# A decoder layer on one core: GpSimd's long arithmetic moved to VectorE, and the delta rule's inverse begun from blocks of 16 rows

## The chip, the core and the metric

The kernel runs on 1 core of one Trainium2 chip. Its engines are TensorE (PE; PEld is its weight load), VectorE (DVE), ScalarE (ACT), GpSimd (POOL), and SyncE (SP), which here issues nearly all DMAs. What counts is the device time of one execution in microseconds (us), the median of several runs. Beside it stands one execution taken by the hardware profiler, from which all rows below come.

## What is computed

One layer of a decoder trunk, 512 tokens of width 1024, in float32: a SwiGLU feed-forward network (FFN), a mixer of two head groups (forgetting attention, "fox", 8 heads of 64, and a gated delta rule, 4 heads of 128), cross-attention to 256 memory tokens, and a second FFN; RMS norms stand before and after each part. The part that the change touches most is the delta rule. Cut to that:

```python
qkv = causal_conv_silu(concat([gq, gk, gv]), conv_w)      # y[t] = sum_i x[t-3+i] * w[i], then silu
decay = exp(where(incl, g[..., :, None] - g[..., None, :], -inf))
L = where(strict, einsum('bhncd,bhnsd->bhncs', k_beta, k) * decay, 0.0)
A = L + eye(CHUNK)                                        # lower triangular, ones on the diagonal
u = triangular_solve(A, v_beta); w = triangular_solve(A, k_beta * exp(g)[..., None])
# scan over the chunks of tokens, with the state S of each head:
v_new = u - w @ S;  o = (q * exp(g)) @ S + attn_intra @ v_new;  S = S * exp(g_last) + k_tail.T @ v_new
```

The kernel takes chunks of 128 tokens and forms T = (I + L)^-1 and its transpose X.

## The kernel before

**Tiling.** Activations stand transposed, [channel, token], in blocks of 128 rows by 512 tokens. A float32 product is made of three passes: every weight block of 128 x 1024 is loaded into a `raw` buffer (three of them), split into a high part `wh` (ScalarE) and a low part `wl` (VectorE, one subtraction with both inputs in SBUF), and TensorE multiplies high by high, high by low and low by high. `wblock` and `wsplit` do that; with `nblock[1] = 2`, which is set from the delta rule to the end of the fox heads and again in the memory attention, every second `wl` is made by GpSimd.

**The mixer.** First come the gates (`zr`, `gw`, `yd`: a softplus worked out by some twenty small VectorE instructions on 128 x 64) and the keys of the four delta heads. `conv` makes the causal convolution of a block: ScalarE writes the first tap (`cy`) and the last (`cth`), VectorE adds two taps, GpSimd adds `cth`, ScalarE takes the tanh, VectorE the product (`co`). Then L of each head is worked out (`L`).

**The inverse.** T is built from 32-row diagonal blocks. L goes to a DRAM buffer (`dl`), its diagonal blocks come back one block to a partition (`Lb`: 4 heads x 4 chunks x 4 blocks = 64 partitions), and 31 steps of substitution on VectorE (a product into `Wb`, a subtraction from `Tb`) invert all of them at once. The blocks go to a DRAM buffer (`dt`), come back in place as `T`, and `inverse` doubles them twice on TensorE: from 32 to 64 rows (products of 32 x 32) and from 64 to 128 (products of 64 x 64), with `Qs` between the two products of a step. `qv` makes queries and values of a head, `scan` runs over its chunks. `PLAN` lists these stages; `F0` are the fox values.

**The order.** Nothing is issued in the order of the text. `Issue` keeps every instruction with what it reads and writes, gives each an assumed duration (in `add`) and an assumed delay to those that wait for it (`AFTER`), places them forwards and backwards ten times, and hands each engine one fixed order. An assumed duration takes no account of what other engines do at that time. SyncE's DMAs are ordered in the same way.

**Norms.** `rstd_of` makes the factor of a row block by one instruction on VectorE, one on ScalarE and a power on GpSimd.

Of the kernel before, what the change touches and what calls it, by code (L numbers as in the profile page):

```python
# [16 lines left out]
P = 128  # L17
# [9 lines left out]
NSLOT = 51  # L27
# [11 lines left out]
class Issue:  # L39
    """The order in which the engines issue.  # L40

    Every instruction is kept with what it reads and writes. At the end they are placed on the
    engines by a rough cost, backwards and forwards by turns, of those ready the most urgent
    first, and each engine gets its instructions in that order (as dependencies that need no
    semaphore).
    """

    # from the end of an instruction to the start of one that waits for it: on the same engine,
    # on the tensor engine, on another
# [45 lines left out]
    def cells(self, x):  # L95
        """name, pieces touched, rows, free size"""
# [22 lines left out]
    def add(self, ins, unit, op, fp32):  # L119
# [4 lines left out]
        for group, cells_of, size_of in ((ins.ins, reads, sizes[0]), (ins.outs, writes, sizes[1])):  # L124
            for x in group:
# [5 lines left out]
                if name.startswith("psum"):  # L131
                    # one after another on a bank
# [51 lines left out]
    def keep(self, unit):  # L184
        """the last instruction stays behind the last kept one of its engine"""
# [4 lines left out]
    def place(self, edges, waits, urgency, clock=False):  # L190
        """start of each instruction, on each unit the most urgent ready one first"""
# [68 lines left out]
class _Issuer:  # L260
    """an engine whose instructions are kept"""
# [19 lines left out]
def tile_decoder_layer(  # L281
# [23 lines left out]
    cid32: bass.AP,  # L305
# [14 lines left out]
    # slots of [128, 512], handed out by hand  # L320
# [20 lines left out]
    def move(src, dst, n=None):  # L341
        """free slots from one ring to another"""
# [14 lines left out]
    def bank(*ids):  # L357
        """the next PSUM bank of a ring of banks"""
# [20 lines left out]
    # that of some instructions stays as written  # L379
# [49 lines left out]
    nblock = [0, 0]  # L429
# [13 lines left out]
    # the first loads, in the order in which they are needed  # L443
# [28 lines left out]
    def prenorm(src, g, dst):  # L472
        """rms_norm of a block of 128 rows, transposed and split into dst(half, part)."""
# [78 lines left out]
    def residual_epilogue(gidx, weight, nxt, final=False):  # L552
        """evac callback: h += weight * rms_norm(product) * gain; then nxt(t)."""
# [165 lines left out]
    # ================= mixer =================  # L719
# [9 lines left out]
    cr = issue.tile(pool, [P, 11], F32, tag="cr", name="cr")  # L729
# [41 lines left out]
    # gates: each of four groups of 32 rows holds a decay logit, two forget logits and a beta  # L771
    # logit, four rows each, and the same again for the low part of the weights; the logarithms are worked out by token, [128 tok, chunk, group, kind]
# [57 lines left out]
    def aug(src):  # L830
        """rows (-hi, -lo, 1, 1) and (1, 1, hi, lo) of a logarithm, whose product is its difference"""
# [15 lines left out]
    # per-token columns [128 tok, chunk, head]  # L847
# [25 lines left out]
    def conv(blk, ps):  # L873
# [18 lines left out]
    nblock[1] = 2  # L892
# [4 lines left out]
    # the 32-row diagonal blocks of each head go through DRAM, a block to a partition and back  # L897
# [674 lines left out]
```

## Time and profile before

| | |
|---|---|
| median of 3 runs | 1224.75 us (1223.94 to 1227.4) |
| profiled execution, first to last instruction | 1222.4 us |
| median less that span | 2.35 us |
| TensorE busy | 1192.9 us (98%), 6078 products |
| VectorE busy | 642.7 us (53%) |
| ScalarE busy | 493.0 us (40%) |
| GpSimd busy | 128.6 us (11%) |
| mean granted clock of TensorE | 0.995 |

The stages by the time in the span: FFN 1 to about 375 us, the mixer's gates, keys and delta rule to about 555, the fox heads to about 640, output projection and memory attention to about 880, FFN 2 to the end. A line of the profile that is named L270 is the recording helper of the program, so instructions are told apart by the names of what they write and read. Busy time on TensorE counts a product from its start to its modelled end, and products overlap; the distance from one start to the next is what a product costs.

### The profile page before, as it was taken

Reading aid. Unit: us, or ns where it says so; the run is one execution under the profiler, and the core shown is the slowest. Engines: PE = TensorE matmul, PEld = TensorE weight load, DVE = VectorE, ACT = ScalarE, POOL = GpSimd, SP = SyncE. Lnnn points to the kernel's source line nnn. Section 1 sums busy time; section 2 is a strip of 40 time slices with the busy share of each in tenths; the row PEclk is TensorE's granted clock in tenths of the full one; section 3 lists DMA queues with packets and bytes.
Section 4 is the critical chain, followed back from the end, with each engine's and each line's share of the span. In section 5 each row is a group of like instructions: output and inputs, shape, how many; then the busy total and the mean of one; then the engine's idle time right before and its main releaser. Section 6 shows DMA issues by size and latency. Waiting matters only on the chain.

```text
span 1222.4 us, 15630 instructions
## 1 busy us (share of the span) xinstructions
PE 1192.9 (98%) x6078; PEld 1002.6 (82%) x6078; DVE 642.7 (53%) x1152; ACT 493.0 (40%) x1024; POOL 128.6 (11%) x121
## 2 busy tenths in 40 slices
PE   7999999999999899899999999999999999999997
PEld 7888888888888687788787888888988888888886
DVE  5655455442327979469975744546634334342323
ACT  5323223222226564368974644435422323222221
POOL 1000000000001432222020442012000000000000
PEclk9999999999999999999999999999999999999999
DMA  5332322333333231211214253222432332333321
GB/s 192 122 100 90 103 88 102 103 103 104 109 101 104 87 113 57 91 54 54 73 60 164 91 181 118 79 67 65 125 103 88 102 97 93 104 107 100 102 71 69
DMA packets 41753, 120.32 MB, mean 98 GB/s; under 512 B 9424, under 2 KB 9680, under 8 KB 41680
## 3 DMA queue, kind: packets, MB, share of 16 engines
q1 hardware_dynamic: 41168, 119.20, 30.9%
q8 instruction: 47, 0.77, 0.3%
q0 software_dynamic: 512, 0.13, 0.1%
q14 instruction: 26, 0.21, 0.1%
HBM read 114.73 MB, written 4.46 MB: 98 GB/s over the span
## 4 chain that ended last, share of the span: by engine, by line
PE 87%; DVE 7%; DMA 2%; issue 2%; ACT 2%; SPq 0%; POOL 0%; DVEq 0%; POOLq 0%; ACTq 0%
PE psum L270 87%; DVE Wb L270 1%; DVE Tb L270 1%; DMA mr<-in_mem_dram 1%; DVE wl L270 1%; DVE gw L270 1%; DMA raw<-in_wkvk_dram 1%; DVE co L270 1%; DVE xn L270 1%; DVE cy L270 0%; SPq L270 0%; DMA h<-in_x_dram 0%; DVE smalls L270 0%; DVE pt L270 0%; DVE h L270 0%
## 5 line engine op out<-in xcount | busy, mean ns | idle before, releaser
L270 PE MATMUL psum<-xt,wh 128*128 128x512 f32 (+1 forms) x2064 | 599.4, 374 | 0.3 <-ACT wh L270 0.2
L270 PEld LDWEIGHTS psum<-xt,wh 128*128 128x128 f32 x2064 | 373.6, 190 | 63.5 <-ACT wh L270 0.5
L270 ACT ACTIVATE wh<-raw 128x1024 fp32r<-128x1024 f32 (+1 forms) x202 | 213.0, 1056 | 526.0 <-PE psum L270 293.3
L270 PE MATMUL psum<-xt,wl 128*128 128x512 f32 (+1 forms) x1016 | 376.6, 375 | 0.8 <-DVE wl L270 0.7
L270 DVE TENSOR_TENSOR wl<-raw,wh 128x1024 fp32r<-128x1024 f32 (+1 forms) x176 | 216.3, 1230 | 275.8 <-ACT wh L270 275.2
L270 PEld LDWEIGHTS psum<-xt,wl 128*128 128x128 f32 x1016 | 190.9, 190 | 32.7 <-DVE wl L270 1.2
L270 PE MATMUL psum<-wh,hh 128*128 128x512 f32 x352 | 137.1, 390 | 0.0
L270 PE MATMUL psum<-wl,hh 128*128 128x512 f32 x352 | 137.1, 390 | 0.0
L270 PE MATMUL psum<-wh,hl 128*128 128x512 f32 x352 | 137.0, 389 | 0.0
L270 POOL TENSOR_TENSOR smalls<-smalls,mhalf 128x1 f32<-128x1 f32 (+1 forms) x38 | 26.5, 700 | 789.8 <-ACT smalls L270 784.0
L270 PEld LDWEIGHTS psum<-wh,hh 128*128 128x128 f32 x352 | 66.1, 188 | 13.8
L270 PEld LDWEIGHTS psum<-wh,hl 128*128 128x128 f32 x352 | 66.1, 188 | 13.6
L270 PEld LDWEIGHTS psum<-wl,hh 128*128 128x128 f32 x352 | 66.1, 188 | 13.6
L270 POOL TENSOR_TENSOR wl<-raw,wh 128x1024 fp32r<-128x1024 f32 x26 | 63.7, 2450 | 120.8 <-ACT wh L270 110.2
L270 PE MATMUL psum<-wh,xt 128*128 128x512 f32 x128 | 43.5, 409 | 0.4 <-DVE q L270 0.4
L270 DVE SCALAR_TENSOR_TENSOR hv<-s,psum 128x512 f32<-128x512 f32 x22 | 15.1, 688 | 53.7 <-PE psum L270 53.5
L270 DVE TENSOR_TENSOR tu<-psum,rb 128x512 f32<-128x512 f32 x22 | 15.2, 692 | 53.4 <-PE psum L270 53.3
L270 DVE TENSOR_TENSOR fg<-psum,gbc 128x512 f32<-128x512 f32 x32 | 22.0, 688 | 37.1 <-ACT u L270 37.1
L270 DVE TENSOR_TENSOR tg<-psum,rb 128x512 f32<-128x512 f32 x22 | 15.2, 692 | 44.5 <-PE psum L270 44.5
L270 ACT ACTIVATE u<-psum 128x512 f32<-128x512 f32 x32 | 19.0, 593 | 41.4 <-PE psum L270 41.4
L270 ACT ACTIVATE hh<-hv 128x512 fp32r<-128x512 f32 x44 | 27.4, 623 | 16.2 <-DVE hv L270 16.2
L270 DVE TENSOR_TENSOR hl<-hv,hh 128x512 fp32r<-128x512 f32 x44 | 30.1, 685 | 1.5 <-ACT hh L270 1.5
(232 smaller groups left out, 1431.3 us busy)
## 6 DMA issues: line engine op xcount, KB each, us to landing
raw<-in_f2gu_dram SPq DMA_DIRECT2D x44, 512.0 KB
raw<-in_f1gu_dram SPq DMA_DIRECT2D x43, 512.0 KB
raw<-in_f1d_dram SPq DMA_DIRECT2D x22, 512.0 KB
raw<-in_f2d_dram SPq DMA_DIRECT2D x22, 512.0 KB
raw<-in_wmt_dram SPq DMA_DIRECT2D x21, 512.0 KB
gbc<-in_gains_dram SPq DMA_DIRECT2D x16, 256.0 KB
raw<-in_wmn_dram SPq DMA_DIRECT2D x8, 512.0 KB
raw<-in_wout_dram SPq DMA_DIRECT2D x8, 512.0 KB
```

The lines of the kernel that those rows point to most:

```text
L270: r = call(*args, **kw)
```

## The change

- `wblock` gives every low part to VectorE; GpSimd makes none.
- `conv` drops ScalarE's `cth` of the last tap and GpSimd's addition, and VectorE adds three taps instead of two.
- The products with the output gate (`gx`, sixteen of 128 x 128) go from GpSimd to VectorE.
- `rstd_of` drops ScalarE's instruction: VectorE adds both sums and the constant in one.
- The substitution works on blocks of 16 rows, 32 to a head, 128 partitions in all: 15 steps instead of 31, on at most 64 elements a partition instead of 256. `Lb` and `Tb` are moved by one DMA a head instead of four, with rows of 64 bytes instead of 128; `dl`, `dt` and `T` are moved in rows of 512 bytes instead of 2048.
- `inverse` doubles once more, from 16 to 32 rows, ahead of the old steps: per head 16 products into `qp`, a masked copy on VectorE, 28 products into `xp` and 7 subtractions on VectorE.
- In `add`, one-pass products are assumed 10.7 ns longer, four-pass products on at most 32 rows half as long, and the scan instruction on VectorE twice as long an element. Three more slots of SBUF are handed out.

```diff
-            cost = max(size * passes * 0.41667, cols * 0.8333) + 2.6
+            cost = max(size * passes * 0.41667, cols * 0.8333) + (13.3 if passes == 1 else 2.6)
+            if passes == 4 and rows <= 32:
+                cost /= 2
-            cost = 68 + size * (6.3 if op == "reciprocal" else 0.521 if single else 1.042) + 61 * scalars
+            each = {"reciprocal": 6.3, "tensor_tensor_scan": 2.04}.get(op, 0.521 if single else 1.042)
+            cost = 68 + size * each + 61 * scalars
...
-        V.tensor_scalar(z0, s0, EPS, None, ALU.add)
-        A.activation(z, z0, AF.Identity, bias=s1)
+        V.tensor_scalar(z, s0, s1, EPS, ALU.add, ALU.add)
...
-        nblock[0] += 1
-        return wsplit(wload(ap), G if nblock[1] and nblock[0] % nblock[1] == 0 else V)
+        return wsplit(wload(ap))
...
-        A.activation(th[:, 0 : S - 3], ps[:, 0 : S - 3], AF.Copy, scale=w4[:, 0:1])
-        for i in (2, 1):
+        for i in (2, 1, 0):
             d = 3 - i
             V.scalar_tensor_tensor(y[:, d:], ps[:, : S - d], w4[:, i : i + 1], y[:, d:], ALU.mult, ALU.add)
-        G.tensor_tensor(y[:, 3:], y[:, 3:], th[:, 0 : S - 3], ALU.add)
...
-        Q.dma_start(rows_of(dl[hh]), L)
-        for c in range(NT):
-            p0 = 16 * hh + 4 * c
-            Q.dma_start(Lb[p0 : p0 + 4], blocks_of(dl[hh], c))
+        Q.dma_start(rows_of(dl[hh]), by_chunk(L))
+        Q.dma_start(Lb[32 * hh : 32 * hh + 32], blocks_of(dl[hh]))
...
-    for j in range(31):
-        n = [64, 31 - j, j + 1]
+    for j in range(15):
+        n = [P, 15 - j, j + 1]
...
+        quarters = [slice(32 * i, 32 * i + 32) for i in range(4)]
+        qp = pg()
+        for c in range(NT):
+            for b in quarters:
+                mm(qp[b, 32 * c : 32 * c + 32], ck(L, c)[b, b], ck(X, c)[b, b], start=True, stop=True)
+        V.tensor_tensor(c3(Qs[:, 0:P]), c3(qp[:, 0:P]), low16[:, None, :].to_broadcast([P, NT, 32]), ALU.mult)
+        xp = pg()
+        for c in range(NT):
+            for b in quarters:
+                mm(xp[b, 32 * c : 32 * c + 32], ck(T, c)[b, b], Qs[b, 32 * c : 32 * c + 32], start=True, stop=True)
+            for b in quarters[0:3]:
+                mm(xp[b, P + 32 * c : P + 32 * c + 32], Qs[b, 32 * c : 32 * c + 32], ck(T, c)[b, b], start=True, stop=True)
+        for i, b in enumerate(quarters):
+            V.tensor_tensor(c3(X)[b, :, b], c3(X)[b, :, b], c3(xp[:, 0:P])[b], ALU.subtract)
+            if i < 3:
+                V.tensor_tensor(c3(T)[b, :, b], c3(T)[b, :, b], c3(xp[:, P : 2 * P])[b], ALU.subtract)
...
-            G.tensor_tensor(ck(gx, c), ck(oraw[hh], c), ck(sgz[c], hh), ALU.mult)
+            V.tensor_tensor(ck(gx, c), ck(oraw[hh], c), ck(sgz[c], hh), ALU.mult)
```

The three places at which the order is looked at follow. On VectorE, the end of the gates (`gw` up to `yd`, which TensorE transposes next); before:

```order
L270 SCALAR_TENSOR_TENSOR cy_458_3102<-psum_64,cw_2744,cy_458_3102 128x511
L270 SCALAR_TENSOR_TENSOR gw_430_2964<-gw_430_2964 128x64
L270 SCALAR_TENSOR_TENSOR cy_458_3102<-psum_64,cw_2744,cy_458_3102 128x510
L270 SCALAR_TENSOR_TENSOR gw_430_2964<-gw_430_2964 128x64 x7
L270 TENSOR_TENSOR gw_430_2964<-gw_430_2964 128x64
L270 TENSOR_TENSOR gw_430_2964<-gw_430_2964,coef_2750 128x64
L270 SCALAR_TENSOR_TENSOR co_460_3110<-cth_459_3104,cy_458_3102 128x512
L270 COPY yd_431_2988<-gw_430_2964 128x16x16
```

and after:

```order
L273 SCALAR_TENSOR_TENSOR gw_430_2952<-gw_430_2952 128x64
L273 TENSOR_TENSOR wl_518_3513<-raw_516_3510,wh_517_3512 128x1024
L273 SCALAR_TENSOR_TENSOR gw_430_2952<-gw_430_2952 128x64
L273 SCALAR_TENSOR_TENSOR cy_487_3320<-psum_64,cw_2732,cy_487_3320 128x511
L273 TENSOR_TENSOR gw_430_2952<-gw_430_2952 128x64
L273 SCALAR_TENSOR_TENSOR cy_487_3320<-psum_64,cw_2732,cy_487_3320 128x510
L273 TENSOR_TENSOR gw_430_2952<-gw_430_2952,coef_2738 128x64
L273 SCALAR_TENSOR_TENSOR co_478_3219<-cth_477_3214,cy_476_3212 128x512
L273 COPY yd_431_2976<-gw_430_2952 128x16x16
```

The seven dependent `gw` instructions that stood in a row have convolutions and weight splits between them, and the convolutions run further ahead (three heads of keys and the first query). On GpSimd, the first stage of the mixer, from the cleared buffer `zb` on; before:

```order
L270 MEMSET zb_448_3040 128x512
L270 TENSOR_TENSOR cy_450_3050<-cy_450_3050,cth_451_3052 128x509
L270 TENSOR_TENSOR wl_487_3353<-raw_485_3350,wh_486_3352 128x1024
L270 TENSOR_TENSOR cy_458_3102<-cy_458_3102,cth_459_3104 128x509
L270 TENSOR_TENSOR wl_503_3465<-raw_501_3462,wh_502_3464 128x1024
L270 TENSOR_TENSOR smalls_63<-smalls_63,mhalf_66 128x4
```

and after:

```order
L273 MEMSET zb_448_3028 128x512
L273 TENSOR_TENSOR smalls_63<-smalls_63,mhalf_66 128x4 x4
L273 DMA k2_618_4530<-ao_603_4448 4x512
L273 TENSOR_TENSOR ro_538_3755<-smalls_63,mhalf_66 128x4
L273 TENSOR_TENSOR ro_546_3897<-smalls_63,mhalf_66 128x4
```

What is left on GpSimd there are powers on four columns, memory fills and DMA issues. On TensorE, the first products of the inverse (X, L, Qs and T of a head; `wh`, `wl` with `xt` are the fox values); before:

```order
L270 MATMUL psum_64<-wh_572_4046,xt_390_2564 128x512
L270 MATMUL psum_64<-X_534_3692,L_457_3092 32x32 x4
L270 MATMUL psum_64<-wh_575_4076,xt_389_2563 128x512
L270 MATMUL psum_64<-wl_576_4077,xt_389_2563 128x512
L270 MATMUL psum_64<-wh_575_4076,xt_390_2564 128x512
L270 MATMUL psum_64<-wh_575_4076,xt_389_2563 128x512
```

and after:

```order
L273 MATMUL psum_64<-wh_565_4016,xt_387_2556 128x512
L273 MATMUL psum_64<-X_533_3623,L_456_3079 32x32 x16
L273 MATMUL psum_64<-wl_566_4017,xt_387_2556 128x512
L273 MATMUL psum_64<-X_541_3765,L_464_3127 32x32 x14
L273 MATMUL psum_64<-Qs_534_3625,T_532_3621 32x32 x4
L273 MATMUL psum_64<-T_532_3621,Qs_534_3625 32x32 x3
L273 MATMUL psum_64<-Qs_534_3625,T_532_3621 32x32 x4
```

The first inverse starts in the first block of the fox values, where it stood in the fourth and last one, and the first two heads go side by side.

## Rows read from the trace of the kernel before

**Rows 1.** Windows: stretch, us, busy us and count by engine, granted clock, DMA.

```profile
395.00:415.00 20.00, 15.95 (x100) 14.23 (x99) 18.54 (x39) 9.69 (x22) 9.61 (x6) 0.91 0.34 106
415.00:435.00 20.00, 18.74 (x106) 14.83 (x105) 17.85 (x45) 15.86 (x57) 8.38 (x6) 1.00 0.26 83
...
455.00:475.00 20.00, 17.37 (x81) 13.94 (x80) 19.22 (x35) 9.59 (x28) 5.77 (x4) 0.91 0.25 79
...
495.00:502.00 7.00, 4.04 (x18) 3.00 (x16) 1.52 (x2) 1.06 (x1) 1.74 (x1) 1.00 0.32 69
502.00:520.00 18.00, 17.64 (x177) 14.12 (x178) 7.87 (x23) 8.96 (x32) 0.60 (x1) 0.91 0.32 107
...
680.00:720.00 40.00, 37.88 (x273) 35.16 (x272) 29.37 (x36) 24.94 (x46) 18.96 (x11) 1.00 0.43 143
...
920.00:1100.00 180.00, 180.00 (x796) 149.05 (x795) 72.60 (x85) 51.61 (x66) 0.00 (x0) 1.00 0.32 100
```

**Rows 2.** Waits of TensorE: waited for, us in total, times, longest.

```profile
PE psum L270 <- DVE smalls L270: 4.6, 2, 4.0
...
PE psum L270 <- DVE X L270: 3.3, 1, 3.3
...
PE psum L270 <- ACT vb L270: 2.6, 1, 2.6
```

**Rows 3.** Timeline of 393 to 415: start, us, engine, instruction, idle before.

```profile
397.02 3.00 POOL L270 TENSOR_TENSOR wl<-raw,wh 128x1024 fp32r<-128x1024 f32 x1 [0.34 <-ACT wh L270]
...
397.93 2.17 DVE L270 SCALAR_TENSOR_TENSOR gw<-gw 128x64 f32<-128x64 f32 x1
...
403.78 0.22 DVE L270 SCALAR_TENSOR_TENSOR gw<-gw 128x64 f32<-128x64 f32 x1
...
403.91 0.74 DVE L270 SCALAR_TENSOR_TENSOR cy<-psum,cw,cy 128x510 f32<-128x510 f32 x1
...
404.57 4.75 DVE L270 SCALAR_TENSOR_TENSOR gw<-gw 128x64 f32<-128x64 f32 x7
...
410.80 1.08 PE L270 MATMUL psum<-ident,yd 128*128 128x128 f32 x4 [4.05 <-DVE smalls L270]
```

**Rows 4.** Timeline of VectorE: two steps of substitution, first transpose of T, a norm.

```profile
449.72 0.21 DVE L270 TENSOR_TENSOR Tb<-Tb,Wb 64x60 f32<-64x60 f32 x1
449.97 0.24 DVE L270 TENSOR_TENSOR Wb<-Lb,Tb 64x87 f32<-64x87 f32 x1
...
457.39 2.46 DVE L270 TENSOR_TENSOR Wb<-Lb,Tb 64x207 f32<-64x207 f32 x1
...
501.55 0.71 DVE L270 STREAM_TRANSPOSE X<-T 128x512 f32<-128x512 f32 x1 [5.48 <-DMA T<-dt]
...
694.70 1.42 DVE L270 SCALAR_TENSOR_TENSOR xn<-h,smalls,gbc 128x512 f32<-128x512 f32 x2 [0.44 <-POOL smalls L270]
...
705.41 3.50 DVE L270 SCALAR_TENSOR_TENSOR xn<-h,smalls,gbc 128x512 f32<-128x512 f32 x2
```

**Rows 5.** Groups of VectorE from 395 to 502: count, busy us, mean ns.

```profile
L270 DVE TENSOR_TENSOR Wb<-Lb,Tb 64x31 f32<-64x31 f32 (+15 forms) x31 | 16.3, 527 | 0.7
L270 DVE TENSOR_TENSOR Tb<-Tb,Wb 64x31 f32<-64x31 f32 (+15 forms) x31 | 13.6, 440 | 0.6
L270 DVE TENSOR_TENSOR wl<-raw,wh 128x1024 fp32r<-128x1024 f32 x8 | 10.1, 1264 | 0.0
```

**Rows 6.** SyncE's timeline after the last substitution step.

```profile
494.96 3.80 SPq L270 DMA_DIRECT2D dt<-Tb  x9
```

**Rows 7.** TensorE's timeline: products of 32 x 32 in the old inverse.

```profile
506.02 0.21 PE L270 MATMUL psum<-Qs,T 32*32 32x32 f32 x1
...
506.70 0.51 PE L270 MATMUL psum<-wl,xt 128*128 128x512 f32 x1
...
509.89 0.43 PE L270 MATMUL psum<-Qs,T 32*32 32x32 f32 x8
510.26 0.50 PE L270 MATMUL psum<-wl,xt 128*128 128x512 f32 x1
```

More of the change, by code (lines that the diff above doesn't have):

```diff
@@ L26 @@
 NEG = -1.0e30
-NSLOT = 51
+NSLOT = 54
 NSMALL = 128
@@ L304, in tile_decoder_layer @@
     crow: bass.AP,
-    cid32: bass.AP,
+    cid16: bass.AP,
     out: bass.AP,
@@ L415, in rstd_of @@
         z = small(1)
-        z0 = small(1)
-        V.tensor_scalar(z0, s0, EPS, None, ALU.add)
-        A.activation(z, z0, AF.Identity, bias=s1)
+        V.tensor_scalar(z, s0, s1, EPS, ALU.add, ALU.add)
         r = small(1)
@@ L728, in tile_decoder_layer @@
     identR, mstrict, minclT, mdiag = (cm[:, i * P : (i + 1) * P] for i in range(4))
-    cr = issue.tile(pool, [P, 11], F32, tag="cr", name="cr")
+    cr = issue.tile(pool, [P, 43], F32, tag="cr", name="cr")
     QK.dma_start(cr, crow)
@@ L748, in tile_decoder_layer @@
     sel = cr[:, 7:11]
+    low16 = cr[:, 11:43]
     w_first = [wblock(wmt[i]) for i in range(4)]
@@ L895, in tile_decoder_layer, with blocks_of, by_chunk @@
         move("m", r_, n_)
-    NB = 32 * S + 32
+    NB = 16 * P + 16
+    NC = 8 * NB
     def rows_of(buf):
-        return buf.rearrange("b x -> (b x)")[0 : P * S].rearrange("(p q) -> p q", q=S)
-    def blocks_of(buf, c):
-        return buf[:, 0 : 32 * S].rearrange("b (r q) -> b r q", q=S)[:, :, c * P : c * P + 32]
-    dl = [issue.tile(dram, [4, NB], F32, tag="dl", bufs=4, name=nm("dl"), grain=(0, 32)) for _ in range(GH)]
-    dt_ = [issue.tile(dram, [4, NB], F32, tag="dt", bufs=4, name=nm("dt"), grain=(0, 32)) for _ in range(GH)]
+        return buf.rearrange("c (p q) -> p c q", q=P)[0:P]
+    def blocks_of(buf):
+        flat = buf.rearrange("c x -> (c x)").rearrange("(i x) -> i x", x=NB)
+        return flat[:, 0 : 16 * P].rearrange("i (r q) -> i r q", q=P)[:, :, 0:16]
+    dl = [issue.tile(dram, [4, NC], F32, tag="dl", bufs=4, name=nm("dl"), grain=(0, NC)) for _ in range(GH)]
+    dt_ = [issue.tile(dram, [4, NC], F32, tag="dt", bufs=4, name=nm("dt"), grain=(0, NC)) for _ in range(GH)]
+    def by_chunk(t_):
+        return t_.rearrange("p (c q) -> p c q", c=NT)
     zb = u(s="zb")
@@ L910, in tile_decoder_layer @@
     for hh in range(GH):
-        Q.dma_start(rows_of(dt_[hh]), zb)
+        Q.dma_start(rows_of(dt_[hh]), by_chunk(zb))
     fr(zb)
-    Lb, Tb = (issue.tile(pool, [P, D], F32, tag=t_, name=t_, grain=(4, 1024))[0:64].rearrange("p (r s) -> p r s", r=32) for t_ in ("Lb", "Tb"))
-    Wb = u(s="Wb")
-    QK.dma_start(Tb, cid32.rearrange("p (r s) -> p r s", r=32))
+    Lb, Tb = (
+        issue.tile(pool, [P, 256], F32, tag=t_, name=t_, grain=(32, 256)).rearrange("p (r s) -> p r s", r=16)
+        for t_ in ("Lb", "Tb")
+    )
+    Wb = issue.tile(pool, [P, 64], F32, tag="Wb", name="Wb")
+    QK.dma_start(Tb, cid16.rearrange("p (r s) -> p r s", r=16))
     def banks(hh):
@@ L1041, in inverse @@
         L = front[hh][1]
-        for c in range(NT):
-            p0 = 16 * hh + 4 * c
-            Q.dma_start(blocks_of(dt_[hh], c), Tb[p0 : p0 + 4])
+        Q.dma_start(blocks_of(dt_[hh]), Tb[32 * hh : 32 * hh + 32])
         T = u(s="T", ring=gr)
-        Q.dma_start(T, rows_of(dt_[hh]))
+        Q.dma_start(by_chunk(T), rows_of(dt_[hh]))
         X = u(s="X", ring=gr)
         V.transpose(X, T)
-        def c3(t_):
-            return t_.rearrange("p (c q) -> p c q", c=NT)
+        c3 = by_chunk
         Qs = u(s="Qs", ring=gr)
+        quarters = [slice(32 * i, 32 * i + 32) for i in range(4)]
[14 more added lines that the diff above has]
+                V.tensor_tensor(c3(T)[b, :, b], c3(T)[b, :, b], c3(xp[:, P : 2 * P])[b], ALU.subtract)
         qp = pg()
@@ L1061, in inverse @@
                 mm(qp[up, 32 * c : 32 * c + 32], ck(L, c)[dn, up], ck(X, c)[dn, dn], start=True, stop=True)
-            A.activation(Qs[up, 0:P], qp[up, 0:P], AF.Copy)
+            A.activation(Qs[up, P : 2 * P], qp[up, 0:P], AF.Copy)
         xp = pg()
@@ L1066, in inverse @@
             for c in range(NT):
-                mm(xp[up, 32 * c : 32 * c + 32], ck(T, c)[up, up], Qs[up, 32 * c : 32 * c + 32], start=True, stop=True)
+                mm(xp[up, 32 * c : 32 * c + 32], ck(T, c)[up, up], Qs[up, P + 32 * c : P + 32 * c + 32], start=True, stop=True)
                 if i == 0:
@@ L1070, in inverse @@
                         xp[dn, P + 32 * c : P + 32 * c + 32],
-                        Qs[up, 32 * c : 32 * c + 32],
+                        Qs[up, P + 32 * c : P + 32 * c + 32],
                         ck(T, c)[up, up],
@@ L1263, in tile_decoder_layer @@
         fr(*p_)
-    nblock[1] = 0
     sgz = [None] * NT
@@ L1327, in tile_decoder_layer @@
     )
-    nblock[1] = 2
     def mk(k, q_, sl=slice(0, 256)):
@@ L1442, in tile_decoder_layer @@
     )
-    nblock[1] = 0
     acc_ids[0] = (0, 1, 2, 3, 4, 5)
@@ L1460, in _consts @@
     cmask = np.concatenate([ident, mstrict, minclT, mdiag], axis=1)
-    crow = np.zeros((P, 11), np.float32)
+    crow = np.zeros((P, 43), np.float32)
     crow[:, 0:1] = np.where(r % 16 < 4, 1.0, -1.0)
@@ L1471, in _consts @@
         crow[32 * m, 7 + m] = 1.0
-    cid32 = np.ascontiguousarray(np.broadcast_to(np.eye(32, dtype=np.float32).reshape(1, 1024), (64, 1024)))
-    return cmask, crow, cid32
+    crow[:, 11:43] = (r % 32 < 16) & (np.arange(32)[None, :] >= 16)
+    cid16 = np.ascontiguousarray(np.broadcast_to(np.eye(16, dtype=np.float32).reshape(1, 256), (P, 256)))
+    return cmask, crow, cid16
 def kernel(**inputs):
@@ L1535 @@
     )
-    cmask, crow, cid32 = _consts(np)
+    cmask, crow, cid16 = _consts(np)
     arrs = dict(
@@ L1558 @@
         crow=crow,
-        cid32=cid32,
+        cid16=cid16,
     )
```

5 lines of the change are left out of this document (1 added, 4 removed).

## The prediction

> **What bounds the kernel now.** I read the shares first: TensorE is busy for 98% of the span, so the time is its work plus its waits, and a change elsewhere counts only where TensorE waits. In FFN 2, where nothing waits, 796 products fill 180.00 us, 226 ns each [rows 1]; neither FFN has anything to gain. The windows then show where TensorE is not busy and where its clock is not 1.00: only in the mixer and around the norm ahead of the memory attention. From 395 to 415 it is idle for 4.05 us, from 415 to 435 for 1.26, from 455 to 475 for 2.63, from 495 to 520 for 2.96 + 0.36, from 680 to 720 for 2.12: 13.4 us. Three of these windows have a clock of 0.91 [rows 1]: the engine falls to 1.2 GHz for a while after each of the three long waits and back to 2.4, and 0.09 of 20, 20 and 18 us, 5.2 us of work, is lost so. That is 18.6 us in all. Some 2 us more are spread over the fox heads.
>
> Next: who keeps TensorE waiting. The waits name VectorE's work for the gates (4.0 us at once; the transposes of `yd` end it), the first `X`, and `vb`, a product of VectorE's chain of convolutions [rows 2, 3]. VectorE in turn is held by GpSimd. A `gw` instruction of 0.22 us takes 2.17 while a GpSimd weight split of 3.00 us runs, and seven of them in a row take 4.75, where 7 x 0.22 is 1.5 [rows 3]. The same happens to a substitution step (2.46 us, where others take 0.21 and 0.24) and to the two `xn` of a norm, 3.50 us together where two others take 1.42 [rows 4]. So the long GpSimd instructions don't help VectorE in the mixer; they stop it for as long as they run, wherever its instruction has both inputs in SBUF.
>
> **The change, part by part.**
>
> *Gates.* Before, TensorE has 54 products of 256 columns, 17 of 512 and a few transposes between the transposes of `zr` and those of `yd`: 54 x 0.12 (half of 226 ns, rounded up) + 17 x 0.226 + 1.1 = 11.4 us. It then waits 4, so VectorE takes over 15. After, the order puts 70 products of 512 columns and four transposes there, 70 x 0.226 + 1.1 = 17.0 us, and forty VectorE instructions: 10 taps, 3 `co`, 3 splits, 24 small ones. By their durations that is 7.4 + 2.0 + 3.7 + 5.7 = 18.8 us; but independent instructions overlap by 0.08 us (`cy` takes 0.74, the next starts 0.66 later, [rows 3]), which leaves 15.5. With 0.75 us ahead of the first of them the wait is 0 to 2.6 us. I keep 0.5 of the 4.05, and drop the 1.8 us of clock that follow: gain 5.3.
>
> *The waits for `co` and `vb`* (1.26 and 2.63 us, with 1.8 us of clock behind the second). Each stands right behind a blocked VectorE instruction; `vb` waited for convolutions queued behind the step of 2.46 us. I expect 0.7 of this 5.7 to stay: gain 5.0.
>
> *Substitution.* 31 steps take 16.3 + 13.6 = 29.9 us of VectorE [rows 5]. A step's half on 60 elements takes 0.21 us and its follower starts 0.25 later [rows 4]; the new halves have 15 to 64 elements, so 30 x 0.25 = 7.5 us. Against the 22 us freed stand 11 added taps by 0.74 (8 us) and 8 splits by 1.26 taken over from GpSimd (10 us, [rows 5]). VectorE's work in this stretch therefore hardly falls; what falls is the time in which it stands blocked, about 20 us. Counted by starts, VectorE needs 49 us from `yd` to the first `X`, and TensorE has 278 products and transposes worth 56.5 us there (177 x 0.226 and 101 smaller ones of 0.16 on average). This slack of 7.5 us has to cover two round trips through DRAM: out with `dt` and back with `T` took 6.6 us before (494.96 to 501.55, [rows 4, 6]), of which nine issues took 3.80, where now four stand instead of sixteen; the order puts 4.3 us of other VectorE work behind the last step, and 3.6 ahead of the first one, where L goes out and back. I count 1 to 3.5 us of waits of VectorE, within the slack. TensorE waited 3.3 us, and 1.6 us of clock were lost behind; 1.5 us I keep for latencies that the slack doesn't cover: gain 3.4.
>
> *The norm at 705.* The block on `xn` (2.1 us) goes: gain 1.9. GpSimd's sixteen splits in the memory attention return to VectorE, 16 x 1.26 us beside over 200 us of TensorE's work in which this block was the only long wait: nothing. `gx` on VectorE, sixteen instructions of a quarter of a tap's size, in a place where TensorE has products of the output projection to do: nothing. ScalarE's instruction in `rstd_of` (0.29 us) lies on a path only in the norms and in the tail, where VectorE's queue takes part of it back: nothing. Of the 2 us spread over the fox heads I take 0.8.
>
> *The extra doubling* is TensorE's own work and hidden by nothing: 44 products a head, 176. Their price is bounded by the old ones: on one tile, four products (8 instructions) take 0.37 us, 92 ns each; where two or three tiles work at a time, the 32 instructions from 506.02 to 506.70, sixteen products, 42 ns each [rows 7]. Four tiles, which the new loops go round, would halve that: 21 ns. So 3.7 to 16.2 us; the order shows all four tiles in turn, so I take 3.7, and 1.6 us for eight more passages into and out of such groups (about 0.1 us at an end, [rows 7]): 5.3 us. Its 7 subtractions and a copy a head, 32 instructions of at most 0.3 us (a substitution half of half the size takes 0.21), fall where VectorE was busy for 7.87 of 18 us [rows 1]; the doubling's latency, a few of these in a row, lies beside another head's and the fox values. If it didn't, the wait of about 2 us would come twice, since the heads go in pairs.
>
> The page TensorEngine Tiling (Array Packing), section Key Properties, of the Trainium skill says that changing the tiling mode drains TensorE, which speaks against this part. It gives no duration; the rows show a passage of about 0.1 us, and if a drain cost the 0.39 us of a full product, eight passages in and eight out would take some 6 us in place of 1.6.
>
> *Sum.* 1222.4 - 5.3 - 5.0 - 3.4 - 1.9 - 0.8 + 5.3 = 1211.3 us of span. The median lies 2.35 us over the profiled span, so **1213.6 us**.
>
> **The rivals.**
>
> *B: the latencies take the waits' place.* The assumed DMA delay of the order is rough, and the rows through DRAM become smaller (64 bytes, and 512 in place of 2048). If the first `X` is late as before (4.9 us instead of my 1.5) and the gates wait for the full 2.6 with 1.0 us of clock behind (instead of 0.5), 6.5 us come back: 1220. For it: VectorE's sum by durations; against: the slack of 7.5 us. The page DMA: Bandwidth & Descriptors of the Trainium skill, section Specifications, wants at least 512 B a transfer for the full rate, below which the engine reads, modifies and writes; the halved 64-byte rows speak for B by that, and no row here shows what a 64-byte row costs.
>
> *C: the small products don't overlap.* At 92 ns they cost 16.2 us, at my other terms 1213.6 + 12.5 = 1226: no change that can be seen. For it: rows at 92 ns exist. Against: these are runs on one tile, and the new order alternates.
>
> *D: slower.* TensorE falls to 1.2 GHz through the inverses. The order spreads them over 38.6 us of TensorE's work; half of that at half the clock adds 19.3 us: 1233. It decides from 15 us of work at the lower level on. For it: the clock drops of 0.91 come exactly where TensorE does little; against: from 506 on the old inverses ran among fox values and no wait followed.
>
> **How the numbers follow.** Mine has a chance of 0.58, B 0.22, C 0.14, D 0.06; 1213.6 is that of the first. Its own range is 1206 (all 18.6 + 2 us gone, the products at 21 ns and no passages: 1222.4 - 20.6 + 3.7 + 2.35 = 1207.9, less 2 for a better order elsewhere) to 1218. With B the range reaches to 1222, which leaves out C and D, 0.2. A difference of 0.3% is 3.7 us, about what a measurement can tell from none: faster means under 1221.1, slower over 1228.4. Faster is mine and B but for its upper edge, 0.8; the same is C, with a little of its neighbours, 0.14; slower is D, 0.06.
>
> **What would show it.** No VectorE instruction with two SBUF inputs takes 2 us in the mixer; `yd` costs TensorE under 1 us, and no window there has a clock of 0.91. The last `Tb` comes some 45 us after `yd` is made. The first X, L products start at about 477 us instead of 502 (the transposes of `zr` at 401.8, since 54 products move ahead of them, and 75 us). The 32 x 32 products advance by about 20 ns each. I am wrong if TensorE still waits 3 us for X, if these products come one behind the other at 90 ns, or if VectorE's longer queue makes TensorE wait in the fox heads.

## The result, and the profile after

The changed kernel takes 1210.94 us (median of 4 runs, 1209.52 to 1211.12), the kernel before beside it 1224.35 (4 runs): a ratio of 0.9883, 95% interval 0.9861 to 0.9905, 13.4 us less. The forecast was 1213.6 us. The profiled execution spans 1207.7 us, where 1222.4 were before; TensorE is busy for 1193.6 us of it (1192.9 before), so it is idle for 14.1 us instead of 29.5, and its mean clock is 0.998 instead of 0.995. VectorE's busy time hardly changes (648.4 us, 642.7 before) although GpSimd's falls from 128.6 to 48.2.

Windows of the changed kernel (columns as in [rows 1]: stretch, us, busy us and count of PE, PEld, DVE, ACT, POOL, granted clock, DMA share, GB/s):

```profile
400.00:420.00 20.00, 20.00 (x98) 16.58 (x97) 19.70 (x50) 10.14 (x22) 2.06 (x1) 1.00 0.35 114
420.00:440.00 20.00, 20.00 (x110) 15.94 (x108) 17.71 (x45) 14.69 (x54) 4.84 (x3) 1.00 0.27 75
...
460.00:480.00 20.00, 20.00 (x266) 16.09 (x266) 15.80 (x39) 8.01 (x14) 0.00 (x0) 1.00 0.39 101
480.00:500.00 20.00, 19.93 (x200) 16.61 (x199) 10.71 (x33) 9.15 (x34) 0.00 (x0) 1.00 0.18 54
500.00:520.00 20.00, 20.00 (x334) 15.01 (x333) 14.25 (x43) 9.53 (x36) 5.61 (x9) 1.00 0.21 57
680.00:700.00 20.00, 19.73 (x166) 19.53 (x165) 16.17 (x21) 11.42 (x17) 0.55 (x1) 1.00 0.71 213
```

Where [rows 1] had idle times of 4.05, 1.26, 2.63, 3.3 and 2.12 us and three windows at a clock of 0.91, TensorE is now idle for no more than 0.07 us (480 to 500) and 0.27 us (680 to 700), at 1.00. What is left of its waits (waited for, us in total, times, longest) lies at the start and, in small pieces, in the fox heads and at the norms; the entries of `smalls`, `X` and `vb` in [rows 2] are gone:

```profile
PE psum L273 <- DMA ident<-in_cmask_dram: 3.7, 1, 3.7
PE psum L273 <- DMA h<-in_x_dram: 1.4, 2, 0.8
PE psum L273 <- DVE q L273: 0.6, 2, 0.4
PE psum L273 <- DVE xn L273: 0.5, 2, 0.3
```

The gates on VectorE and the transposes on TensorE that wait for them (start, us, engine, instruction):

```profile
401.58 0.22 DVE L273 COPY gw<-psum 128x64 f32<-128x64 f32 x1
...
410.70 0.23 DVE L273 SCALAR_TENSOR_TENSOR gw<-gw 128x64 f32<-128x64 f32 x1
410.84 0.75 DVE L273 SCALAR_TENSOR_TENSOR cy<-psum,cw,cy 128x510 f32<-128x510 f32 x1
411.50 0.22 DVE L273 SCALAR_TENSOR_TENSOR gw<-gw 128x64 f32<-128x64 f32 x1
...
416.69 0.29 DVE L273 COPY yd<-gw 128x256 f32<-128x256 f32 x1
...
417.15 0.60 PE L273 MATMUL psum<-ident,yd 128*128 128x128 f32 x4
```

Each `gw` takes 0.22 us (2.17 beside a GpSimd split in [rows 3]); the longest VectorE instruction between 395 and 850 us is a weight split of 1.23. The transposes of `yd` start without an idle time where [rows 3] had 4.05.

The substitution, first VectorE's groups of 395 to 480 (count, busy us, mean ns, idle before):

```profile
L273 DVE TENSOR_TENSOR Wb<-Lb,Tb 128x15 f32<-128x15 f32 (+7 forms) x15 | 3.1, 204 | 0.3
L273 DVE TENSOR_TENSOR Tb<-Tb,Wb 128x15 f32<-128x15 f32 (+7 forms) x15 | 3.0, 203 | 0.3
```

then the timeline: the last step, SyncE's move of the blocks, the first transposes, and TensorE's first small products:

```profile
467.67 0.17 DVE L273 TENSOR_TENSOR Tb<-Tb,Wb 128x15 f32<-128x15 f32 x1
...
467.87 1.92 SPq L273 DMA_DIRECT2D dt<-Tb  x4
...
473.79 1.30 DVE L273 STREAM_TRANSPOSE X<-T 128x512 f32<-128x512 f32 x2
...
474.84 0.61 PE L273 MATMUL psum<-wh,xt 128*128 128x512 f32 x2
475.38 0.45 PE L273 MATMUL psum<-X,L 32*32 32x32 f32 x32
475.77 0.49 PE L273 MATMUL psum<-wl,xt 128*128 128x512 f32 x1
```

The steps take 6.1 us where [rows 5] had 29.9, and from the last `Tb` to the first transpose of T it takes 5.95 us (467.84 to 473.79; 6.6 before, [rows 4, 6]), most of which VectorE fills with other work. Sixteen products, 32 instructions, fill 475.38 to 475.77.

One thing about this profiled execution: the first rows of `x` came early. TensorE waited 1.4 us for `h` (3.1 in the profile before, 0.2 to 2.9 in the others of this study), and the change touches nothing there. With the wait for `ident`, its start cost 5.1 us against 6.5 before, so of the 14.7 us between the two spans some 1.4 are this start, which leaves 13.3, about the 13.4 of the medians. The other runs of the changed kernel span 1209.0 to 1209.3 us. In the experiments below, one of the six runs of A + C took 1702.57 us at a mean granted clock of 0.655, a slow state of the chip, and is left out.

### The profile page after: what moved, and what is told of

Same layout as the page of the kernel before. It is cut to its first block, busy times and chain, and to the rows that moved or that the text cites. A ratio compares the mean times of both kernels' runs of the same rounds, so it can differ in the third digit from the quotient of the medians.

```text
span 1207.7 us, 16266 instructions
## 1 busy us (share of the span) xinstructions
PE 1193.6 (99%) x6430; PEld 1001.2 (83%) x6430; DVE 648.4 (54%) x1206; ACT 478.9 (40%) x978; POOL 48.2 (4%) x67
## 4 chain that ended last, share of the span: by engine, by line
PE 90%; DVE 5%; ACT 2%; issue 1%; DMA 1%; POOL 1%; SPq 0%; DVEq 0%; POOLq 0%; ACTq 0%
PE psum L273 90%; DVE h L273 1%; DVE xn L273 1%; DVE wl L273 1%; POOL smalls L273 1%; DVE p L273 1%; DVE xt L273 1%; ACT wh L273 1%; ACT u L273 1%; DVE pt L273 0%; DMA h<-in_x_dram 0%; ACT k L273 0%; DVE smalls L273 0%; DMA raw<-in_wkvk_dram 0%; ACT p L273 0%
## 5 line engine op out<-in xcount | busy, mean ns | idle before, releaser
L273 DVE TENSOR_TENSOR wl<-raw,wh 128x1024 fp32r<-128x1024 f32 (+1 forms) x202 | 246.6, 1221 | 277.7 <-ACT wh L273 276.5
L273 PEld LDWEIGHTS psum<-wh,hl 128*128 128x128 f32 x352 | 66.1, 188 | 13.6
L273 POOL TENSOR_TENSOR smalls<-smalls,mhalf 128x1 f32<-128x1 f32 (+1 forms) x38 | 31.0, 815 | 687.0 <-DVE smalls L273 686.7
L273 ACT ACTIVATE hh<-hv 128x512 fp32r<-128x512 f32 x44 | 27.4, 624 | 17.1 <-DVE hv L273 17.1
L273 PEld LDWEIGHTS psum<-wh,xt 128*128 128x128 f32 x128 | 23.4, 189 | 4.3 <-DVE q L273 0.6
```

Source lines behind the costliest of these rows:

```text
L273: r = call(*args, **kw)
```

## The experiments

The change has three parts. A: no long arithmetic on GpSimd (weight splits, additions of the convolution, `gx`, and the shorter `rstd_of`). B: blocks of 16 rows. C: the new assumed durations. My theory was that A brings the gain, because a long GpSimd instruction holds up VectorE's instructions with two SBUF inputs and TensorE then waits for them. Rival 1: B brings it, by the 22 us that it takes off VectorE. Rival 2: C, by a better order. All eight combinations were timed, each ratio against runs of the kernel before on the same chip. "Idle" is the profile's span less TensorE's busy time; "held" is, over VectorE's instructions that overlap one of GpSimd, the time above the lower quartile of instructions of the same form, where that is over 0.05 us. "Clock" is the mean granted clock of the profiled run.

| kernel | median us | ratio, 95% interval | idle us | clock | held us |
|---|---|---|---|---|---|
| before | 1224.35 | 1 | 29.5 | 0.995 | 26.6 |
| A (a_alone) | 1212.47 | 0.9901 (0.9884 to 0.9918) | 16.4 | 0.992 | 0.7 |
| B (b_alone) | 1222.17 | 0.9987 (0.9971 to 1.0002) | 24.0 | 0.997 | 22.3 |
| C (c_alone) | 1235.48 | 1.0078 (1.0046 to 1.0111) | 33.1 | 0.985 | 25.7 |
| A + B (ab) | 1215.90 | 0.9933 (0.9912 to 0.9953) | 20.1 | 0.999 | 0.7 |
| A + C (ac) | 1214.8 | 0.9909 (0.9887 to 0.9932) | 18.7 | 0.994 | 0.7 |
| B + C (bc) | 1234.54 | 1.0078 (1.0062 to 1.0095) | 33.2 | 0.994 | 24.8 |
| A + B + C (the change) | 1210.94 | 0.9883 (0.9861 to 0.9905) | 14.1 | 0.998 | 0.7 |

**A alone.** The kernel before, with

```diff
-        nblock[0] += 1
-        return wsplit(wload(ap), G if nblock[1] and nblock[0] % nblock[1] == 0 else V)
+        return wsplit(wload(ap))
```

and the edits of `conv`, `gx` and `rstd_of` as in the change.

> The kernel before, with GpSimd's weight splits, additions of the convolution and gx on VectorE and the shorter rstd_of; 32-row blocks and the old assumed durations stay. Theory (VectorE stands blocked beside long GpSimd instructions, and that makes TensorE wait): the waits of the gates, of co and vb and of the norm go, 5.9 + 5.7 + 1.9 + 0.8 us, the wait for the first X with its clock stays at up to 4.9, and no doubling is added: 1210 us, at most 1213. Rival 1 (the gain comes from the 22 us of substitution that the 16-row blocks take off VectorE): VectorE has 18 us more to do and no relief, TensorE waits 5 us or more for the first X, 1220 or over. Rival 2 (the gain comes from the order that the new assumed durations give): 1220 or over.

1212.47 us: 12 of the 13.4 us come from A, against both rivals. Its waits of TensorE:

```profile
PE psum L270 <- DMA h<-in_x_dram: 2.3, 1, 2.3
PE psum L270 <- ACT vb L270: 1.2, 2, 0.9
PE psum L270 <- ACT wh L270: 0.6, 1, 0.6
PE psum L270 <- DVE q L270: 0.5, 1, 0.5
PE psum L270 <- ACT Qs L270: 0.5, 1, 0.5
```

The wait for the first X (3.3 us in [rows 2]) is not among them, although the old 31 steps are still there and X, L starts at 493.4 us, 18 us later than in the changed kernel. The order puts fox values ahead of it.

A alone has a loss of its own that its waits don't show. Its windows behind the first inverses:

```profile
510.00:521.00 11.00, 9.31 (x92) 7.66 (x91) 10.17 (x27) 9.79 (x37) 4.53 (x7) 1.00 0.48 145
521.00:538.10 17.10, 17.10 (x109) 14.08 (x109) 8.54 (x19) 6.67 (x19) 0.00 (x0) 0.50 0.20 63
```

After 1.69 us of idle time in three pieces of 0.25 to 0.95, TensorE works for 17.1 us at 1.2 GHz, which costs about 8.5 us (half of it, an estimate from these rows). All five runs of A have a mean clock of 0.990 to 0.992. So the 12 us of A are what is left after this loss.

**A + C**, the changed kernel with the old blocks and the two old doublings:

```diff
-    for j in range(15):
-        n = [P, 15 - j, j + 1]
+    for j in range(31):
+        n = [64, 31 - j, j + 1]
```

> The changed kernel without the 16-row blocks: no long GpSimd arithmetic, new assumed durations, 32-row blocks and two doublings. Theory: the 5.6 us of TensorE's extra products go, and the first X comes later by up to 22 us of VectorE's work, of which the order can hide some behind fox values; 1206 to 1212, so level with the changed kernel or better. Rival 1 (the 16-row blocks carry the gain): TensorE waits over 5 us for the first X and the kernel is at 1217 or over. Rival 2 (order): 1206 to 1212 as well, but then a_alone is at 1220.

1214.8 us, 3 over my range and under rival 1's. By the overlapping intervals it can't be told from the changed kernel, nor A alone from either. Its five runs fall in two groups that go with the granted clock: 1210.7 and 1211.13 us at 0.998 and 0.997, as the changed kernel, and 1214.8 to 1217.44 at 0.992 to 0.994. The profile is of the second group and shows the stretch of A alone again, shorter:

```profile
520.40:530.60 10.20, 10.20 (x69) 7.96 (x69) 3.98 (x10) 2.88 (x9) 0.00 (x0) 0.50 0.18 51
```

The profiles of the two kernels with A and the new blocks (A + B and the change) show no such stretch in the mixer. So what the new blocks bring next to A seems to be less the freed VectorE than TensorE's clock in the inverses; whether the blocks themselves or the order around them keep it up isn't shown.

**B alone**, and **B + C**, the changed kernel with GpSimd's arithmetic put back (B alone has the old assumed durations as well):

```diff
-        return wsplit(wload(ap))
+        nblock[0] += 1
+        return wsplit(wload(ap), G if nblock[1] and nblock[0] % nblock[1] == 0 else V)
...
-        for i in (2, 1, 0):
+        A.activation(th[:, 0 : S - 3], ps[:, 0 : S - 3], AF.Copy, scale=w4[:, 0:1])
+        for i in (2, 1):
...
+        G.tensor_tensor(y[:, 3:], y[:, 3:], th[:, 0 : S - 3], ALU.add)
```

`gx`, `rstd_of` and the settings of `nblock[1]` are put back likewise.

> The kernel before with nothing but the 16-row blocks (and the slots of SBUF that they free). Theory: VectorE stays blocked at the gates, co, vb and the norm, the wait for the first X (4.9 us with the clock) may go, and the small products cost 4 us, or 8 where the old assumed durations let two heads alternate on one tile, as they did without the new durations before: 1222 to 1233. Rival (the freed 22 us of VectorE carry the gain): 1211 to 1218.

> The changed kernel with GpSimd's arithmetic put back (every second weight split from the delta rule on, the addition of the convolution, gx, and the longer rstd_of). Theory: instructions of VectorE with two SBUF inputs take 2 to 3 us again beside the splits, TensorE waits for the gates, co, vb and the norm as before, 14 us with the clock, only the wait for the first X (4.9) is gone and 5.6 us of products are there: 1222 to 1227. Rivals 1 and 2 (the blocks, or the order, carry the gain): 1211 to 1216.

B alone gives 1222.17, not to be told from before: rival 1 is out. B + C gives 1234.54, 7 us over the top of my range. Its longest waits of TensorE:

```profile
PE psum L273 <- DVE xn L273: 5.7, 2, 4.6
...
PE psum L273 <- DVE yd L273: 3.3, 1, 3.3
PE psum L273 <- DVE co L273: 3.3, 3, 1.5
PE psum L273 <- DVE smalls L273: 2.5, 2, 2.3
```

Of the names in [rows 2], `smalls` is back and X is not; `vb` has 0.7 us left. The norm and `co` are back too, at more than twice their length in the kernel before:

```profile
PE psum L270 <- DVE xn L270: 2.1, 2, 1.9
PE psum L270 <- DVE co L270: 1.3, 1, 1.3
```

I had taken every wait over at its old length.

**C alone**, and **A + B** (the changed kernel with the old assumed durations), both by

```diff
-            cost = max(size * passes * 0.41667, cols * 0.8333) + 2.6
+            cost = max(size * passes * 0.41667, cols * 0.8333) + (13.3 if passes == 1 else 2.6)
+            if passes == 4 and rows <= 32:
+                cost /= 2
```

and the line for VectorE, or their reverse.

> The kernel before with nothing but the new assumed durations. Theory: every blocked instruction stays, and no term of the gain is touched: 1221 to 1228. Rival (the order by the new durations carries a good part of the gain): 1212 to 1219.

> The changed kernel with the old assumed durations. Theory: within 2 us of the changed kernel, 1209 to 1213, since no wait depended on 11 ns a product. Rival 2 (the order by the new durations carries the gain): 1217 or over, with waits of TensorE of 2 us or more in the mixer.

Both expectations failed. C alone makes the kernel slower by 11 us (median 1235.48); on top of A + B it makes it faster by 5 (1215.90 to 1210.94; the intervals don't overlap). Rival 2 is out, since C alone gains nothing, but the order matters more than I thought. Waits and two windows of C alone:

```profile
PE psum L273 <- DVE xn L273: 5.2, 2, 4.2
PE psum L273 <- DVE yd L273: 5.0, 1, 5.0
...
PE psum L273 <- ACT vb L273: 3.1, 2, 2.1
...
PE psum L273 <- DVE cy L273: 2.2, 1, 2.2
```

```profile
400.00:420.00 20.00, 15.05 (x61) 12.00 (x60) 19.41 (x41) 8.55 (x21) 7.71 (x5) 0.83 0.31 105
...
480.00:520.00 40.00, 36.13 (x206) 26.51 (x205) 19.89 (x41) 11.89 (x25) 6.41 (x4) 0.74 0.24 73
```

VectorE is held for no longer than before (25.7 us against 26.6), but TensorE waits longer for it, and its mean clock over the 40 us from 480 on, in which it waits 1.7 us for the first X, falls to 0.74. Of the 13.6 us between this profile and the one before, 3.6 are idle time and 10.0 are busy time of TensorE, most of it from the clock: 34 us of the mixer and the norm run at 1.2 GHz instead of 10. Not every run of C has that: two of the five, at a mean clock of 0.994 and 0.995, took 1230.98 and 1229.55 us, the three others, at 0.985 and 0.986, 1235.48 to 1237.92. The order is planned without the delays by GpSimd, so where they fall is left to chance. That reading fits the four pairs with and without A: A gains 11.9 us on before, 6.3 on B, 20.7 on C and 23.6 on B + C, always much and never the same. It isn't shown step by step. For A + B the waits name `pt` (2.1 us), X (1.8), `wh` (1.0) and `wl` (1.0), each under 0.4 us in the changed kernel, and no GpSimd instruction holds VectorE: there the old durations simply give a worse order.

**Which part of GpSimd's work.** The changed kernel with the splits alone put back (the first lines of the diff of B + C, and `nblock[1]` set as before):

> The changed kernel with only the weight splits put back: GpSimd makes every second wl from the delta rule to the end of the fox heads and in the memory attention. Theory (the loss grows with the length of the GpSimd instruction: 0.4 us on an instruction of VectorE beside 0.6 us of GpSimd, 2.0 beside a split of 3.0): the splits are nearly all of it, and the time comes near to that of the kernel with all of GpSimd's arithmetic put back, 1222 to 1234. Rival (the additions of the convolution, gx and rstd_of matter as much, being on paths that TensorE waits for): 1211 to 1217.

1224.03 us, ratio 1.0004 (0.9989 to 1.0020), 13 us over the changed kernel, with 15.0 us held; TensorE waits for `xn` (2.9 us), `pt` (2.9) and `q` (1.5). So the splits alone undo the whole gain. No wait of TensorE there is for a split that GpSimd made late: all but 0.2 us of those in the mixer and behind it are for results of VectorE. But the rest (additions, `gx`, `rstd_of`) adds another 10.5 us to B + C, its interval apart from this one: "nearly all of it" was wrong.

**Is it contention, or GpSimd's late results?** The changed kernel with instructions on GpSimd that nobody needs, behind the clearing of `zb`; the other engines' orders stay the same row by row.

```diff
     QK.dma_start(Tb, cid16.rearrange("p (r s) -> p r s", r=16))
+    by_in = f(cm[:, 0:256]).rearrange("p (r s) -> p r s", r=16)
+    issue.extra = zb_at, [nc.gpsimd.tensor_tensor(Lb, by_in, by_in, ALU.subtract).ins for _ in range(32)]
```

by_mem has 64 times `memset(Lb, 0.0)` there, by_copy 36 times `tensor_copy(Lb, by_in)`.

> The changed kernel with 32 idle subtractions of 128 x 256 on GpSimd, two SBUF inputs each, started behind the clearing of zb at 387 us and written to a buffer that nobody reads before it is overwritten; the other engines' orders are the same, row by row. At 0.6 us each (half of the 1.09 of 128 x 509 before) they fill 387 to 407. Theory (long GpSimd reads of SBUF hold up VectorE's instructions with two SBUF inputs): such instructions (wl, gw, co) grow by up to 0.6 us each in this stretch, some 5 to 10 us of VectorE in all, yd is made later and TensorE waits for it: 1213 to 1221. Rival (before, what hurt was that GpSimd's own results came late): nobody waits for these, 1210 to 1212, and gw stays at 0.22 us.

> The same with 64 memory fills of 128 x 256 on GpSimd, which read nothing; 0.3 us each (half of the 0.53 of 128 x 512), so the same stretch. If any SBUF traffic of GpSimd holds up VectorE: as the idle subtractions, 1213 to 1221. If only its reads do: 1210 to 1212, with gw at 0.22 and wl at 1.23 us throughout. The Trainium skill, page SBUF — State Buffer, section Who interferes with whom, says that an instruction of VectorE with two SBUF inputs contends with a GpSimd instruction that reads SBUF and not with one that only writes it; by it this kernel is at 1210 to 1212.

> The same with 36 copies of 128 x 256 on GpSimd, one SBUF input each, about 0.55 us (twice the 0.29 of the 128 x 128 copy before). If a single read of GpSimd suffices, as the idle subtractions, 1213 to 1221; if it takes two, 1210 to 1212.

The idle subtractions cost 3.9 us (1214.87; ratio 0.9906, 0.9887 to 0.9926); the fills nothing (1210.48), the copies nothing (1210.62). Beside each other on one chip, the four runs with subtractions (1214.1 to 1215.23) lie over all eight of the two others (1209.39 to 1211.5). GpSimd's timelines of the three, in this order:

```profile
387.33 28.06 POOL L927 TENSOR_TENSOR Lb<-cm 128x256 f32<-128x256 f32 x32
```

```profile
387.99 23.71 POOL L926 MEMSET Lb<- 128x256 f32 x64
```

```profile
387.62 20.35 POOL L927 COPY Lb<-cm 128x256 f32<-128x256 f32 x36
```

VectorE's timeline beside the subtractions, and TensorE's wait behind them:

```profile
403.54 0.21 DVE L277 TENSOR_TENSOR gw<-psum,gw 128x64 f32<-128x64 f32 x1
...
404.33 0.47 DVE L277 SCALAR_TENSOR_TENSOR gw<-gw 128x64 f32<-128x64 f32 x1
...
407.30 0.63 DVE L277 TENSOR_TENSOR gw<-gw 128x64 f32<-128x64 f32 x1
...
413.46 0.63 DVE L277 SCALAR_TENSOR_TENSOR gw<-gw 128x64 f32<-128x64 f32 x1
...
416.40 0.16 DVE L277 TENSOR_TENSOR smalls<-smalls 128x4 f32<-128x4 f32 x1 [0.65 <-POOL smalls L277]
```

```profile
PE psum L277 <- DVE yd L277: 2.5, 1, 2.5
```

and the window behind:

```profile
415.00:435.00 20.00, 17.55 (x77) 13.40 (x75) 17.22 (x40) 8.17 (x22) 1.37 (x2) 0.91 0.18 55
```

The same `gw` that takes 0.22 in the changed kernel takes up to 0.63, with nobody reading GpSimd's result; the one with an input in PSUM stays at 0.21. Paired one by one with the changed kernel, VectorE's instructions grow by 2.7 us in all beside the subtractions (I had expected 5 to 10), 0.65 beside the copies, 0.1 beside the fills. A GpSimd power that stands behind the subtractions comes late too and costs VectorE 0.65 us more. So of the 3.4 us by which `yd` is made later, counted from the clearing of `zb`, 2.7 are held instructions and 0.65 the rival's share, a late result; behind the fills the same power ends 1.5 us later instead of 5.8 and delays nothing. TensorE then waits 2.5 us for `yd`, and its clock is at 0.91 in that window, where the changed kernel has 1.00 (0.09 of 20 us, 1.8). This is the chain that the prediction read out of [rows 3], made on purpose.

The page SBUF — State Buffer of the Trainium skill, section Who interferes with whom, says that a VectorE instruction with two SBUF inputs contends with a GpSimd instruction that reads SBUF, not with one that only writes it. The three runs agree: 2.7 and 0.65 us for the readers, 0.1 for the writer. The copies' time of 1210.62 falls where I had put the case that it takes two reads of GpSimd, but one read suffices: VectorE's instructions do grow beside the copies, by too little to reach TensorE. One held instruction has a single SBUF input: a `TENSOR_SCALAR` on `gw` takes 0.60 us beside the subtractions and 0.36 beside the fills, where the changed kernel has 0.19.

**The price of the small products.** The changed kernel with the new doubling's loops the other way round:

```diff
-        for c in range(NT):
-            for b in quarters:
+        for b in quarters:
+            for c in range(NT):
...
```

The two kinds of products into `xp` are each turned in the same way.

> The changed kernel with the new doubling's products issued tile by tile (all four chunks of a 32-row block, then the next block) in place of block by block within a chunk. Theory (products on one and the same 32 x 32 tile come one behind the other at 92 ns, on four tiles in turn at 20): the 172 products in runs on one tile cost 12 us more of TensorE, 1220 to 1224. Rival (the order of the tiles doesn't matter, 20 ns is the price of any such product): 1210 to 1212.

1213.90 us (0.9900, 0.9880 to 0.9920): 3 us more, not 12; the fills, timed beside it, took 1210.48. The first sixteen products, which the changed kernel starts at 475.38, in TensorE's timeline of this kernel:

```profile
476.20 0.89 PE L273 MATMUL psum<-X,L 32*32 32x32 f32 x32
477.02 0.49 PE L273 MATMUL psum<-wl,xt 128*128 128x512 f32 x1
```

They fill 0.82 us to the next full product, where the four tiles in turn take 0.39. From first to last start that is 45 ns a product against 17 (0.70 and 0.26 us for 15.5 steps); in the longer groups it is 38 to 42 and 18 to 19. So the theory had the sign right, and sharing a tile doubles the price, but 92 ns was never the price of a product.

**Would more turns help?** The changed kernel with the old step from 32 to 64 rows written the same way:

```diff
-        for i in range(2):
-            up, dn = slice(64 * i, 64 * i + 32), slice(64 * i + 32, 64 * i + 64)
-            for c in range(NT):
+        for c in range(NT):
+            for up, dn in pairs:
...
```

> The changed kernel with the second doubling (32 to 64 rows) written so that its 80 products go round two or three tiles, as the new doubling's go round four. In the changed kernel they advance by 36 ns (in longer groups) to 69 ns (in groups of four). Theory (the price is set by whether neighbours share a tile): they advance by 20 to 30 ns, 1 to 3 us less of TensorE, 1208.5 to 1210.5. Rival (the price of a short group is its passage, and the number of groups stays): 1210.5 to 1212, no change.

No: 1212.45 us (0.9908, 0.9891 to 0.9925). Its products do advance by 22 to 24 ns where they alternate, and all small groups together, with their passages, take 9.7 us of TensorE instead of 10.6. But the order around them moves too (the last product of `scan` starts at 544.8 us instead of 538.3), and nothing of it is left.

## Why the prediction came out right

**The mechanism** was read correctly: blocked VectorE instructions, waits behind them, the lower clock behind the waits. A alone brings 12 of 13.4 us, and the idle subtractions reproduce it in small. That the sum came within 3 us is in part luck: with the old assumed durations, which no term of it tells apart from the new ones, the same mechanism gives 1215.9.

**Gates.** Predicted: 0.5 of the 4.05 us stays, the clock's 1.8 comes back, 5.3. Measured: nothing stays, 5.9. TensorE starts `yd` 16.8 us after `zr` (17.0 forecast), and VectorE needs 15.4 us from its first `gw` copy to the end of `yd` (15.5 forecast).

**co and vb.** Predicted 5.0; both waits and the clock are gone, 5.7.

**First X.** Predicted 3.4 of 4.9; all of it is gone. X, L starts at 475.4 us (477 forecast, 75.0 us after `zr` as worked out), and the last `Tb` comes 50.7 us after `yd` is made (about 45 forecast). Here the reason was wrong in part: I credited this term to the substitution, and A alone removes the wait as well, with the old steps. Rival B, that the latencies through DRAM take the place of the wait, did not come about: 5.95 us, hidden. Rival D, the lower clock through the inverses, did not come about in the changed kernel either (1.00 from 400 to 520), but it was no empty rival: A alone ran 17.1 us there at 1.2 GHz.

**Norm.** Predicted 1.9; 0.27 us is left of 2.12 (the window 680 to 700), so 1.85.

**gx** was costed at nothing. The window 640 to 660 before had 0.84 us of idle time, 0.7 of it in waits for `ml`, which stands behind `gx`; after, 620 to 660 has none. A small gain overlooked.

**Fox heads.** I took 0.8; the idle time is 1.27 us before (560 to 620) and 1.21 after (540 to 600): nothing.

**The extra doubling.** Predicted 3.7 us for the products and 1.6 for eight passages, 5.3. Measured from TensorE's timeline, starts of neighbours: within the groups 6.35 us against 3.35 before, so 3.0 for the 176 new products, 17 to 19 ns each in the first groups (21 forecast). Sixteen groups stand instead of ten, each with some 0.1 to 0.2 us going in and 0.12 coming out: 1.4. In all 4.4. The upper bound of this term was mis-sized: 0.37 us for four products in [rows 7] is mostly their passage, and rival C, built on 92 ns a product, could not have cost more than the 3 us that the loops the other way round cost.

**The switch of tiling** that the prediction weighed from the page TensorEngine Tiling (Array Packing), section Key Properties, of the Trainium skill, comes to 0.2 to 0.3 us for a group's way in and out together; the 6 us that a drain of a full product would have cost are not there.

**The sum.** Forecast span 1211.3, measured 1207.7. Of the 3.6 us between, 2.7 are the remainders I kept of the gates, of co and vb, and of X; 1.4 are the early start; 0.9 the cheaper doubling; 0.8 `ml`; against that 0.8 that the fox heads did not give. That would be 5.0; the other way 1.4 us are spread over rows that I can't assign. The median lies 3.2 us over this profiled span instead of 2.35, as the profiled run was the fastest of the four (1209.52 us).

**What the prediction left out** is the order. It took the new assumed durations as part of the order shown and gave them no term. They are worth 5 us here, and minus 11 without A, mostly through TensorE's clock: had the change been C alone, my method, which counts held instructions, would have forecast no change. Whether B pays cannot be settled from these runs: it gains 3.9 us on A + C, loses 3.4 on A, and both are about what a measurement tells apart; two runs of A + C are as fast as the changed kernel.

## What to carry to other kernels

Offloading elementwise work to GpSimd was a loss here, where VectorE works at the same time on operands in SBUF. In another kernel, look for VectorE instructions of one form with very different durations, and for GpSimd reads beside them, before counting busy shares. A planned order is only as good as its durations, and a delay that it doesn't know (here 25 us of held VectorE) costs whatever the place makes of it: about the same held time went with 29 us of idle TensorE in one order, and with 33 and a lower clock in another. Read the granted clock of every stretch beside the waits: in A alone no wait was over 1 us behind the start, and 17 us still ran at half the clock. Price a short group of small products by its way in and out first, and let neighbouring products use different tiles.

## What the runs showed of the hardware that I had not expected

- GpSimd loses as well: its subtraction of 128 x 256 takes 0.61 us undisturbed and up to 1.71 beside VectorE, and the 32 take 28.06 us, 0.88 each. The fills are hardly affected (23.71 us for 64).
- Copies on GpSimd, which read one input, held VectorE by 0.2 us at most, the subtractions by 0.4, the 3.0 us split of [rows 3] by 2: in these three the loss of one instruction grows with what stands beside it.
- A 32 x 32 float32 product advances by 17 ns on four tiles in turn, by 38 to 45 on one.
- DMA rows of 64 bytes and of 512 instead of 128 and 2048 did not make a round trip through DRAM longer (5.95 us, 6.6 before); the number of issues fell from sixteen to four at the same time, so the rows' own price isn't shown.
- TensorE fell to 1.2 GHz for 17.1 us behind three idle pieces that add up to 1.69 us among small products (A alone), and did not where the inverses left 0.07 us of idle time from 480 to 520 (the changed kernel).
